# A skewness kernel on one core: fixed engine orders, 31 input transfers instead of 27, the last block's squares in PSUM, seven blocks closed together on GpSimd

## Chip, cores, metric

One Trainium2 chip (trn2), one core. The time is device microseconds (us) of one execution; the span is the time from the first to the last instruction in the trace. A program on one core has shown two kinds of run here: the runs of one kernel on one chip agree within 0.4%, except that one run of one experiment was 2% longer at a lower granted TensorE clock; it is left out of every comparison.

## The reference

```python
rows, cols = 1024, 8192                       # float32
mean = np.mean(x, axis=-1, keepdims=True)
std  = np.std(x, axis=-1, keepdims=True)
z    = (x - mean) / (std + 1e-8)
out  = np.mean(z ** 3, axis=-1)               # 1024 values
```

With the raw means m1, m2, m3 of x, x squared and x cubed, the result is (m3 - 3 m1 m2 + 2 m1^3) / (m2 - m1^2)^1.5, so one pass over x is enough. ("Moment" below is m2.)

## The kernel before

Eight blocks of 128 rows by 8192 columns stream in, each in several tiles, into SBUF, the core's large on-chip memory; PSUM is the smaller one, which also takes TensorE's results. ScalarE squares a tile and sums the squares (`accum_out`), VectorE multiplies the square by x and sums the cubes (such an instruction is called a cube below), TensorE transposes each 128x128 piece into one PSUM tile that adds them up, which gives the row sums.

```python
UNITS = [                       # widths of the transfers of each block: 27 in all
    [4096, 4096], [4096, 4096], [4096, 4096], [4096, 4096],
    [3584, 2304, 2304], [2304, 2304, 2048, 1536],
    [1664, 1792, 1920, 1664, 1152],
    [1024, 1024, 1152, 1280, 1408, 1152, 1152],
]
...
nc.sync.dma_start(out=xt, in_=xv[b, :, c0 : c0 + w])           # x tile, 8 buffers
nc.scalar.activation(out=sq, in_=xt[:, s:e], func=AF.Square, scale=s_scale,
                     accum_out=s2u[:, j : j + 1])
cube = sqpool.tile(...) if last_unit else sq                    # cube overwrites its square
nc.vector.scalar_tensor_tensor(out=cube, in0=sq, scalar=1.0, in1=xt[:, s:e],
                               op0=ALU.mult, op1=ALU.mult, accum_out=s3u[:, j : j + 1])
...
# blocks 0 to 5 are closed by six GpSimd steps while block 6 runs;
# blocks 6 and 7 by six small ScalarE steps each (close_on_act), then:
nc.gpsimd.tensor_tensor(out=rr, in0=var2, in1=expo[:, 0 : NB - F], op=ALU.pow)
nc.vector.tensor_reduce(out=num, in_=s3u[:, F * K :]..., axis=X_AXIS, op=ALU.add)
nc.vector.tensor_tensor(out=skew[:, F:NB], in0=num, in1=rr, op=ALU.mult)
nc.sync.dma_start(out=ov, in_=skew)
```

## Time and profile before

| | before |
|---|---|
| time, median of 3 runs | 91.64 us (91.53 to 91.65) |
| span of the profiled run | 89.73 us |
| last input tile landed | 83.56 us |
| result sent | 87.23 us |
| from there to the end of the span | 2.50 us |

I split the span at two places: until the last input tile has landed, from there until the result is sent (the tail), and the end. The first cut is read from the input transfers sent last: start, then time to landing. The second is the start of the output transfer in the timeline.

```profile
L140 SPq DMA_DIRECT2D x<-in_x_dram x1: 328/328/328, 76.1 to 76.1; - x1
...
DMA to landing us min/median/max: 7.5/7.5/7.5
...
87.23 0.35 SPq L193 DMA_DIRECT2D out_dram<-skew  x1
```

The first two lines say: sent at 76.1, landed 7.5 later, so 83.6. The prediction shows the other views (slices, chain, stretches, timeline) and how they are read.

### The profile page before, as it was taken

What the parts mean: (1) busy time and instruction counts of PE and PEld (TensorE: products, weight loads), DVE (VectorE), ACT (ScalarE), POOL (GpSimd) and SP (SyncE); (2) the same over time, 40 slices, a digit from 0 to 9 for tenths busy, and PEclk for the clock granted to TensorE, in tenths of its full rate; (3) what the DMA queues carried; (4) which work ended last, traced back from release to release, by engine and by line L of the source; (5) the groups of instructions that cost most, each with busy time, mean ns of one, the idle gap of its engine ahead of it and who ended that gap; (6) DMA issues with size and microseconds to landing.
All of it is one profiled execution on the core that took longest, in us unless ns stands there. A gap on an engine that the chain in (4) does not pass through costs nothing.

```text
span 89.7 us, 1368 instructions
## 1 busy us (share of the span) xinstructions
PE 64.9 (72%) x504; PEld 59.3 (66%) x504; DVE 72.7 (81%) x80; ACT 72.1 (80%) x106; POOL 11.3 (13%) x14
## 2 busy tenths in 40 slices
PE   0003999892882919989998988888987798969710
PEld 0003999791872909979897977877876787848500
DVE  1000498989999298995999999999999999999970
ACT  6003999699991999859898989978979898999950
POOL 3000000000000000000000000000005999900030
PEclk9999999999999997599999999999999999999998
DMA  3999999999999999999999999999999999994000
GB/s 117 351 424 438 424 431 431 431 431 424 446 416 431 424 438 424 424 438 427 415 409 418 419 427 419 421 415 419 409 414 417 404 413 411 421 412 161 0 0 2
DMA packets 4038, 33.64 MB, mean 375 GB/s; under 512 B 576, under 2 KB 576, under 8 KB 2240
## 3 DMA queue, kind: packets, MB, share of 16 engines
q1 hardware_dynamic: 4032, 33.56, 89.7%
q8 instruction: 4, 0.07, 0.3%
q14 instruction: 2, 0.02, 0.0%
HBM read 33.55 MB, written 0.00 MB: 374 GB/s over the span
## 4 chain that ended last, share of the span: by engine, by line
DMA 73%; ACT 13%; issue 5%; DVE 4%; SPq 1%; PE 1%; DVEq 0%; ACTq 0%
DMA x<-in_x_dram 73%; ACT sq L147 9%; DVE sq L152 3%; ACT sqps L147 1%; ACT same L159 1%; SPq L140 1%; PE s1ps L175 1%; ACT tsb L174 0%; ACT s3u L128 0%; ACT v L127 0%; ACT var L125 0%; DVE num L189 0%; ACT m1sq L124 0%; DVE skew L192 0%; ACT nm L126 0%
## 5 line engine op out<-in xcount | busy, mean ns | idle before, releaser
L152 DVE SCALAR_TENSOR_TENSOR sq<-sq,x 128x2048 f32<-128x2048 f32 (+9 forms) x35 | 70.7, 2071 | 13.4 <-ACT sq L147 13.3
L165 PE MATMUL tp<-ident,x 128*128 128x128 f32 x488 | 62.6, 288 | 17.3 <-DMA x<-in_x_dram 17.2
L165 PEld LDWEIGHTS tp<-ident,x 128*128 128x128 f32 x488 | 57.9, 150 | 20.9 <-DMA x<-in_x_dram 12.7
L147 ACT ACTIVATE sq<-x 128x2048 f32<-128x2048 f32 (+9 forms) x35 | 60.6, 1734 | 10.7 <-DMA x<-in_x_dram 9.9
L110 POOL TENSOR_TENSOR vara<-m2a,m1sqa 128x6 f32<-128x6 f32 x1 | 1.8, 1822 | 67.1 <-DVE m3a L99 67.1
L147 ACT ACTIVATION_READ_ACCUMULATOR sq<-x 128x1 f32 x35 | 6.5, 186 | 0.0
L175 PEld LDWEIGHTS s1ps<-onesn,tsb 128*128 128x128 f32 x16 | 2.4, 188 | 5.2 <-ACT tsb L174 5.2
L175 PE MATMUL s1ps<-onesn,tsb 128*128 128x1 f32 x16 | 3.1, 260 | 3.3 <-ACT tsb L174 3.3
L174 ACT COPY tsb<-tp 128x128 f32<-128x128 f32 x8 | 2.0, 256 | 2.0 <-PE tp L165 2.0
L114 POOL TENSOR_TENSOR rra<-vara,expo 128x6 f32<-128x6 f32 x1 | 3.3, 3267 | 0.0
L159 ACT ACTIVATE same<-x 128x1024 f32<-128x1024 f32 x3 | 3.1, 1041 | 0.0
L152 DVE DVE_READ_ACCUMULATOR sq<-sq,x 128x1 f32 x35 | 2.9, 83 | 0.0
L111 POOL TENSOR_TENSOR m1sq3a<-m1sq3a,vara 128x6 f32<-128x6 f32 x1 | 1.9, 1868 | 0.1
L77 ACT ACT_TABLE_LOAD x1 | 1.3, 1283 | 0.7 <-PEq L208 0.7
L187 POOL TENSOR_TENSOR rr<-var,expo 128x2 f32<-128x2 f32 x1 | 0.7, 702 | 7.7 <-ACT var L125 7.7
L152 DVE SCALAR_TENSOR_TENSOR cube<-sqps,x 128x1152 f32<-128x1152 f32 x1 | 1.4, 1350 | 0.0
L113 POOL TENSOR_TENSOR m3a<-m3a,m1sq3a 128x6 f32<-128x6 f32 x1 | 1.2, 1201 | 0.1
L147 ACT ACTIVATE sqps<-x 128x1152 f32<-128x1152 f32 x1 | 1.1, 1136 | 0.1
L115 POOL TENSOR_TENSOR skew<-m3a,rra 128x6 f32<-128x6 f32 x1 | 1.1, 1069 | 0.1
L124 ACT ACTIVATE m1sq<-s1ps 128x1 f32<-128x1 f32 x2 | 0.3, 171 | 0.5 <-PE s1ps L175 0.5
L75 DVE MEMSET onesn<- 128x1 f32 x1 | 0.1, 59 | 0.8 <-PEq L208 0.8
L112 POOL TENSOR_TENSOR m1sq3a<-m1sq3a,nm1a 128x6 f32<-128x6 f32 x1 | 0.7, 697 | 0.0
(28 smaller groups left out, 6.8 us busy)
## 6 DMA issues: line engine op xcount, KB each, us to landing
x<-in_x_dram SPq DMA_DIRECT2D x8, 2048.0 KB, 23.4
x<-in_x_dram SPq DMA_DIRECT2D x4, 1152.0 KB, 27.9
x<-in_x_dram SPq DMA_DIRECT2D x4, 576.0 KB, 8.6
x<-in_x_dram SPq DMA_DIRECT2D x1, 1792.0 KB, 33.0
x<-in_x_dram SPq DMA_DIRECT2D x2, 832.0 KB, 13.9
x<-in_x_dram SPq DMA_DIRECT2D x1, 1024.0 KB, 21.1
x<-in_x_dram SPq DMA_DIRECT2D x2, 512.0 KB, 10.0
x<-in_x_dram SPq DMA_DIRECT2D x1, 960.0 KB, 13.2
```

What stands on the lines that cost most here:

```text
L77: nc.scalar.activation(out=tiny, in_=onesn, func=AF.Square)
L110: g.tensor_tensor(out=var, in0=m2, in1=m1sq, op=ALU.subtract)
L111: g.tensor_tensor(out=m1sq3, in0=m1sq3, in1=var, op=ALU.add)
L113: g.tensor_tensor(out=m3, in0=m3, in1=m1sq3, op=ALU.add)
L114: g.tensor_tensor(out=rr, in0=var, in1=expo, op=ALU.pow)
L115: g.tensor_tensor(out=skew[:, 0:F], in0=m3, in1=rr, op=ALU.mult)
L147: nc.scalar.activation(out=sq, in_=xt[:, s:e], func=AF.Square, scale=s_scale, accum_out=s2u[:, j : j + 1],)
L152: nc.vector.scalar_tensor_tensor(out=cube, in0=sq, scalar=1.0, in1=xt[:, s:e], op0=ALU.mult, op1=ALU.mult, accum_out=s3u[:, j : j + 1],)
L159: nc.scalar.activation(out=same[:, 0:w_act], in_=xt[:, w - w_act : w], func=AF.Copy, scale=inv_n, accum_out=s1a[:, b : b + 1],)
L165: nc.tensor.matmul(out=tp, lhsT=xt[:, c * P : (c + 1) * P], rhs=ident, start=(k == 0 and c == 0), stop=(c0 == C and c == n - 1), is_transp ...
L174: nc.scalar.copy(out=tsb, in_=tp)
L175: nc.tensor.matmul(out=s1ps[:, b : b + 1], lhsT=tsb, rhs=onesn, start=True, stop=True)
```

## The change

Its intent: engine orders exactly as the program is written; smaller tiles earlier, so that VectorE is not late at the end; a last tile of 512 columns; no TensorE work given to ScalarE; squares of the last block and of the last tile before it in PSUM, where GpSimd can work beside VectorE; one closing for seven blocks. Cut to its core:

```diff
-    [4096, 4096],
-    [4096, 4096],
-    [3584, 2304, 2304],
-    [2304, 2304, 2048, 1536],
-    [1664, 1792, 1920, 1664, 1152],
-    [1024, 1024, 1152, 1280, 1408, 1152, 1152],
+    [3456, 1792, 2944],
+    [2944, 2304, 2944],
+    [2944, 2688, 2560],
+    [1920, 1920, 1792, 1536, 1024],
+    [1536, 1408, 1408, 1152, 1408, 1280],
+    [1152, 1280, 1408, 1280, 1280, 1280, 512],
-S1_ACT = {(0, 0): 1024, (1, 0): 1024, (2, 0): 1024}
+PSUM_FROM = (6, 5)
+PS_MAX, PS_BUFS = 1536, 2
-EARLY = 6
+EARLY = 7
+EARLY_AT = (7, 2)
...
+    ctx.enter_context(tc.manual_schedule(
+        engines={eng.PE, eng.Activation, eng.DVE, eng.Pool, eng.SP}))
...
+    cube = small("cube", PS_MAX)                       # one scratch tile for all PSUM cubes
...
+            if last_unit:
+                nc.scalar.copy(out=tsb, in_=tp)        # ahead of the last square
+                if (b, k) >= PSUM_FROM:
+                    sq = psq.tile([P, PS_MAX], FP, tag="psq", ...)[:, 0 : e - s]
                 nc.vector.scalar_tensor_tensor(
+                    out=cube[:, 0 : e - s] if (b, k) >= PSUM_FROM else sq,
                     in0=sq, scalar=1.0, in1=xt[:, s:e], ...
...
-    (closing of blocks 6 and 7 on ScalarE)
+    g.tensor_tensor(out=m2, in0=m2p, in1=s2u[:, j - 1 : j], op=ALU.add)
+    act(out=m1sq, in_=p1, func=AF.Square)
+    g.tensor_tensor(out=var, in0=m2, in1=m1sq, op=ALU.subtract)
+    g.tensor_tensor(out=rr, in0=var, in1=expo[:, 0:1], op=ALU.pow)
+    act(out=nm1, in_=p1, func=AF.Copy, scale=-3.0)
+    act(out=v3, in_=m1sq, func=AF.Identity, scale=1.0 / 3.0, bias=var)
+    nc.vector.tensor_reduce(out=num, in_=s3u[:, L * K : L * K + n_sl[L]], ...)
+    nc.vector.scalar_tensor_tensor(out=num, in0=v3, scalar=nm1, in1=num, op0=ALU.mult, op1=ALU.add)
+    nc.vector.tensor_tensor(out=skew[:, L:NB], in0=num, in1=rr, op=ALU.mult)
```

More of the change, by code (lines that the diff above doesn't have):

```diff
@@ L17, with _slices, _plan @@
     [4096, 4096],
-    [4096, 4096],
-    [4096, 4096],
-    [3584, 2304, 2304],
-    [2304, 2304, 2048, 1536],
-    [1664, 1792, 1920, 1664, 1152],
-    [1024, 1024, 1152, 1280, 1408, 1152, 1152],
+    [3456, 1792, 2944],
[4 more added lines that the diff above has]
+    [1152, 1280, 1408, 1280, 1280, 1280, 512],
 ]
-S1_ACT = {(0, 0): 1024, (1, 0): 1024, (2, 0): 1024}
+PSUM_FROM = (6, 5)
 SUB_MAX = 2304
+PS_MAX, PS_BUFS = 1536, 2
 X_BUFS = 8
 SQ_BUFS = 4
-EARLY = 6
-def _slices(w):
-    n = -(-w // SUB_MAX)
+EARLY = 7
+EARLY_AT = (7, 2)
+def _slices(w, most):
+    n = -(-w // most)
     step = -(-w // n // 128) * 128
     return [(s, min(s + step, w)) for s in range(0, w, step)]
+def _plan(b, k):
+    return _slices(UNITS[b][k], PS_MAX if (b, k) >= PSUM_FROM else SUB_MAX)
 @with_exitstack
@@ L45 @@
     nc = tc.nc
+    eng = mybir.EngineType
+    ctx.enter_context(tc.manual_schedule(
+        engines={eng.PE, eng.Activation, eng.DVE, eng.Pool, eng.SP}))
     P = nc.NUM_PARTITIONS
@@ L53 @@
     third = (1.0 / 3.0) ** 0.5
-    assert len(UNITS) == NB and all(sum(u) == C for u in UNITS)
-    nw = len(S1_ACT)
-    assert sorted(b for b, _ in S1_ACT) == list(range(nw)) and nw <= F
+    assert len(UNITS) == NB and all(sum(u) == C for u in UNITS) and F == L
     xv = x.rearrange("(p b) c -> b p c", b=NB)
     ov = out.rearrange("(p b) -> p b", b=NB)
-    K = max(sum(len(_slices(w)) for w in u) for u in UNITS) + 1
+    n_sl = [sum(len(_plan(b, k)) for k in range(len(u))) for b, u in enumerate(UNITS)]
+    K = max(n_sl)
     xpool = ctx.enter_context(tc.tile_pool(name="xp", bufs=X_BUFS))
@@ L67 @@
     onep = ctx.enter_context(tc.tile_pool(name="onep", bufs=1))
-    psum = ctx.enter_context(tc.tile_pool(name="ps", bufs=2, space=bass.MemoryType.PSUM))
+    psq = ctx.enter_context(tc.tile_pool(name="psq", bufs=PS_BUFS, space=bass.MemoryType.PSUM))
     psum1 = ctx.enter_context(tc.tile_pool(name="ps1", bufs=1, space=bass.MemoryType.PSUM))
@@ L83 @@
     nc.vector.memset(s3u, 0.0)
-    s1a = small("s1a", nw)
-    same = small("same", max(S1_ACT.values()))
+    cube = small("cube", PS_MAX)
     junk = small("junk", K)
@@ L89 @@
     skew = small("skew", NB)
-    s1ps = psum1.tile([P, NB], FP, tag="s1ps")
     m1a = small("m1a", F)
-    var2 = small("var2", NB - F)
-    Tsb = [small(f"tsb{i}", P) for i in range(2)]
+    tsb = small("tsb", P)
+    tp = psum1.tile([P, P], FP, tag="tp", name="tp")
+    s1ps = psum1.tile([P, NB], FP, tag="s1ps", name="s1ps")
+    act, g = nc.scalar.activation, nc.gpsimd
     def close_first_blocks():
@@ L103, in close_first_blocks @@
         m1sq, m1sq3, nm1 = small("m1sqa", F), small("m1sq3a", F), small("nm1a", F)
-        nc.scalar.copy(out=m1a[:, nw:F], in_=s1ps[:, nw:F])
-        nc.scalar.activation(out=m1sq, in_=m1a, func=AF.Square)
-        nc.scalar.activation(out=m1sq3, in_=m1a, func=AF.Square, scale=third)
-        nc.scalar.activation(out=nm1, in_=m1a, func=AF.Copy, scale=-3.0)
-        g = nc.gpsimd
+        act(out=m1sq, in_=m1a, func=AF.Square)
+        act(out=m1sq3, in_=m1a, func=AF.Square, scale=third)
+        act(out=nm1, in_=m1a, func=AF.Copy, scale=-3.0)
         var, rr = small("vara", F), small("rra", F)
@@ L115, in close_first_blocks @@
         g.tensor_tensor(out=skew[:, 0:F], in0=m3, in1=rr, op=ALU.mult)
-    def close_on_act(b):
-        m2, m1sq, nm1, v3 = (small(f"{t}_{b}", 1) for t in ("m2", "m1sq", "nm1", "v3"))
-        p1 = s1ps[:, b : b + 1]
-        var = var2[:, b - F : b - F + 1]
-        act = nc.scalar.activation
-        yield act(out=junk, in_=s2u[:, b * K : b * K + K], func=AF.Copy, accum_out=m2)
-        yield act(out=m1sq, in_=p1, func=AF.Square)
-        yield act(out=var, in_=m1sq, func=AF.Identity, scale=-1.0, bias=m2)
-        yield act(out=nm1, in_=p1, func=AF.Copy, scale=-3.0)
-        yield act(out=v3, in_=m1sq, func=AF.Identity, scale=1.0 / 3.0, bias=var)
-        yield act(
-            out=s3u[:, b * K + K - 1 : b * K + K], in_=v3, func=AF.Identity, scale=nm1
-        )
-    pending = iter(())
     for b, widths in enumerate(UNITS):
-        tp = psum.tile([P, P], FP, tag="tp", name=f"tp_{b}")
         c0 = 0
@@ L141 @@
             c0 += w
-            for s, e in _slices(w):
-                if last_unit:
-                    sq = psum1.tile([P, e - s], FP, tag="sqps", name=f"sqps_{s}")
-                else:
-                    sq = sqpool.tile([P, e - s], FP, tag="sq", name=f"sq_{b}_{k}_{s}")
-                nc.scalar.activation(
-                    out=sq, in_=xt[:, s:e], func=AF.Square, scale=s_scale,
-                    accum_out=s2u[:, j : j + 1],
-                )
-                cube = sqpool.tile([P, e - s], FP, tag="sq", name="cube") if last_unit else sq
-                nc.vector.scalar_tensor_tensor(
-                    out=cube, in0=sq, scalar=1.0, in1=xt[:, s:e],
-                    op0=ALU.mult, op1=ALU.mult, accum_out=s3u[:, j : j + 1],
-                )
-                j += 1
-            w_act = S1_ACT.get((b, k), 0)
-            if w_act:
-                nc.scalar.activation(
-                    out=same[:, 0:w_act], in_=xt[:, w - w_act : w], func=AF.Copy,
-                    scale=inv_n, accum_out=s1a[:, b : b + 1],
-                )
-            n = (w - w_act) // P
+            n = w // P
             for c in range(n):
@@ L169 @@
                 )
-            if k > 0:
-                next(pending, None)
-                next(pending, None)
-        tsb = Tsb[b % 2]
-        nc.scalar.copy(out=tsb, in_=tp)
-        nc.tensor.matmul(out=s1ps[:, b : b + 1], lhsT=tsb, rhs=onesn, start=True, stop=True)
-        if b == F - 2:
-            nc.vector.tensor_tensor(
-                out=m1a[:, 0:nw], in0=s1ps[:, 0:nw], in1=s1a, op=ALU.add
-            )
-        if b == F - 1:
-            close_first_blocks()
-        if b >= F:
-            pending = close_on_act(b)
@@ L184 @@
-    for _ in pending:
-        pass
-    rr = small("rr2", NB - F)
-    nc.gpsimd.tensor_tensor(out=rr, in0=var2, in1=expo[:, 0 : NB - F], op=ALU.pow)
-    num = small("num2", NB - F)
-    nc.vector.tensor_reduce(
-        out=num, in_=s3u[:, F * K :].rearrange("p (b c) -> p b c", c=K), axis=X_AXIS, op=ALU.add
-    )
-    nc.vector.tensor_tensor(out=skew[:, F:NB], in0=num, in1=rr, op=ALU.mult)
+            if last_unit:
+                nc.scalar.copy(out=tsb, in_=tp)
+            for s, e in _plan(b, k):
+                if (b, k) >= PSUM_FROM:
+                    sq = psq.tile([P, PS_MAX], FP, tag="psq", name=f"psq_{b}_{k}_{s}")[:, 0 : e - s]
+                else:
+                    sq = sqpool.tile([P, e - s], FP, tag="sq", name=f"sq_{b}_{k}_{s}")
+                act(
+                    out=sq, in_=xt[:, s:e], func=AF.Square, scale=s_scale,
+                    accum_out=s2u[:, j : j + 1],
+                )
+                nc.vector.scalar_tensor_tensor(
+                    out=cube[:, 0 : e - s] if (b, k) >= PSUM_FROM else sq,
+                    in0=sq, scalar=1.0, in1=xt[:, s:e],
+                    op0=ALU.mult, op1=ALU.mult, accum_out=s3u[:, j : j + 1],
+                )
+                j += 1
@@ new lines @@
+            if (b, k) == EARLY_AT:
+                nc.scalar.copy(out=m1a, in_=s1ps[:, 0:F])
+                close_first_blocks()
+            if b == L and k == len(widths) - 2:
+                m2p = small("m2p", 1)
+                act(out=junk[:, 0 : n_sl[L] - 1], in_=s2u[:, L * K : j], func=AF.Copy,
+                    accum_out=m2p)
+        if b < L:
+            nc.scalar.copy(out=tsb, in_=tp)
+        nc.tensor.matmul(out=s1ps[:, b : b + 1], lhsT=tsb, rhs=onesn, start=True, stop=True)
@@ new lines @@
+    p1 = s1ps[:, L : L + 1]
+    m1sq, nm1, v3, m2, var, rr, num = (
+        small(f"{t}_l", 1) for t in ("m1sq", "nm1", "v3", "m2", "var", "rr", "num")
+    )
+    g.tensor_tensor(out=m2, in0=m2p, in1=s2u[:, j - 1 : j], op=ALU.add)
[4 more added lines that the diff above has]
+    act(out=v3, in_=m1sq, func=AF.Identity, scale=1.0 / 3.0, bias=var)
@@ L193 @@
+    nc.vector.tensor_reduce(out=num, in_=s3u[:, L * K : L * K + n_sl[L]], axis=X_AXIS, op=ALU.add)
+    nc.vector.scalar_tensor_tensor(
+        out=num, in0=v3, scalar=nm1, in1=num, op0=ALU.mult, op1=ALU.add
+    )
+    nc.vector.tensor_tensor(out=skew[:, L:NB], in0=num, in1=rr, op=ALU.mult)
     nc.sync.dma_start(out=ov, in_=skew)
```

## The prediction

> **What bounds the kernel now.** I read the page first: the 40 slices, then the chain that ended last.
>
> ```profile
> DMA  3999999999999999999999999999999999994000
> GB/s 117 351 424 438 424 431 431 431 431 424 446 416 431 424 438 424 424 438 427 415 409 418 419 427 419 421 415 419 409 414 417 404 413 411 421 412 161 0 0 2
> DMA 73%; ACT 13%; issue 5%; DVE 4%; SPq 1%; PE 1%; DVEq 0%; ACTq 0%
> ```
>
> The 16 DMA engines are full from the second slice to the 36th: the 33.55 MB of x stream in without a gap, and no compute engine ever lets the queue run dry. So the span of 89.7 us is the stream plus what follows its last landing. The chain in order of time gives the cut between the two:
>
> ```profile
> 76.06 7.50 DMA x<-in_x_dram
> 83.56 0.02 issue
> 83.58 1.26 ACT sqps L147 x2
> 84.84 0.28 ACT tsb L174
> 85.12 0.04 issue
> 85.16 0.40 PE s1ps L175 x2
> ...
> 85.81 0.27 ACT var L125
> 86.09 0.02 issue
> 86.11 0.30 ACT v L127
> 86.42 0.02 issue
> 86.44 0.30 ACT s3u L128
> ...
> 87.04 0.16 DVE skew L192
> ```
>
> The last tile (1152 columns) lands at 83.56 us. From there it is 3.67 us until the result is sent (87.23 in the timeline), and 2.5 us more to the end of the span. In the tail, square, copy of the transposes, row sum and the five small ScalarE steps follow one another. Only those 3.67 us and the rate of the stream can change the time.
>
> Third, the rate against the width of the rows, from the stretches of ten microseconds (last column GB/s, the one before it the DMA share):
>
> ```profile
> 8.00:18.00 10.00, 9.42 (x58) 9.21 (x59) 7.47 (x7) 9.06 (x12) 0.00 (x0) 1.00 1.01 433
> 48.00:58.00 10.00, 9.00 (x80) 8.53 (x81) 10.00 (x11) 9.46 (x10) 0.00 (x0) 1.00 1.01 420
> 68.00:78.00 10.00, 8.65 (x74) 7.66 (x73) 10.00 (x15) 9.24 (x19) 9.38 (x6) 1.00 1.02 412
> ```
>
> The engines are equally full in all three, but with 4096-column tiles they move 433 GB/s, with 2304-column ones 420, and with those of 1024 to 1920 columns 412. A smaller transfer costs rate, though nothing waits.
>
> Fourth, the timeline of the end, for the pace of VectorE and for GpSimd:
>
> ```profile
> 68.26 1.88 DVE L152 SCALAR_TENSOR_TENSOR sq<-sq,x 128x1664 f32<-128x1664 f32 x1
> 68.38 1.82 POOL L110 TENSOR_TENSOR vara<-m2a,m1sqa 128x6 f32<-128x6 f32 x1 [67.07 <-DVE m3a L99]
> ...
> 79.72 1.36 DVE L152 SCALAR_TENSOR_TENSOR sq<-sq,x 128x1152 f32<-128x1152 f32 x1
> 81.00 1.49 DVE L152 SCALAR_TENSOR_TENSOR sq<-sq,x 128x1280 f32<-128x1280 f32 x1
> 82.42 1.62 DVE L152 SCALAR_TENSOR_TENSOR sq<-sq,x 128x1408 f32<-128x1408 f32 x1
> 85.24 1.35 DVE L152 SCALAR_TENSOR_TENSOR cube<-sqps,x 128x1152 f32<-128x1152 f32 x1
> 86.16 0.70 POOL L187 TENSOR_TENSOR rr<-var,expo 128x2 f32<-128x2 f32 x1 [7.68 <-ACT var L125]
> ```
>
> Starts of VectorE in a row give its pace: 1.28 us for 1152 columns, 1.42 for 1280, 1.54 for 1408, so about 1.04 ns a column and 0.08 us an instruction. ScalarE's squares, read the same way (starts at 78.45, 79.59, 80.86, 82.27), take 1.14, 1.27 and 1.41. A block of 8192 columns costs VectorE 9.0 us in six slices, and the stream 10.0: VectorE has 10% to spare, and at the end is as late as ScalarE's chain (its cube ends at 86.6, the chain at 86.7).
>
> **What the Trainium skill says.** "DMA: Bandwidth & Descriptors", section Bandwidth: a fixed cost per packet makes small rows slower, and 435 GB/s is the ceiling of the fabric; the trace agrees in kind, 433 falling to 412. The same page, "Queues, rings and completion order": each engine takes turns between queue rows packet by packet, so other traffic delays one engine of the 16; the page of before lists 4 packets of an instruction queue, 0.07 MB, and the stream fades out over two microseconds (161 GB/s in slice 37) instead of stopping at once, which fits, though no view here names the engine. "SBUF — State Buffer", "two separate sides": VectorE with two SBUF inputs and GpSimd exclude each other for whole instructions. The trace agrees: six-element subtractions took 1.8 us and ended 0.06 us after the VectorE instruction beside them (68.38+1.82=70.20 against 70.14). "ScalarE: Activation LUTs", "Step-by-step", holds PSUM the lower-latency destination; here 1136 ns against 1155 for 1152 columns, so 0.02 us, which I count as nothing.
>
> **The change part by part.**
> Stream. 27 input transfers become 31. A block of 4.194 MB takes 9.69 us at 433 GB/s in 2 transfers and 10.18 at 412 in about 5.9 (mean width 1390 in that stretch): 0.49 us for 3.9 transfers, 0.125 each. Four more: +0.5 us; the 420 of the middle stretch would make it a little different, so I take +0.45. Does the queue run dry? The eight transfers sent at once now hold 27,520 columns instead of 32,768. Tile k+8 leaves when tile k is cubed, some 6 us after landing at 4096 columns and 3 us at 1280; what is then still queued is never below about 7,000 columns, 8 us of stream. So no. The last landing moves from 83.56 to about 84.0.
>
> First blocks. Three partial sums on ScalarE go (1.04+0.19 us each); 24 transposes at about 0.12 us come to TensorE, 8 in each of three blocks: 64 x 0.12 = 7.8 us a block of ten. None is on the chain: worth 0. The single transpose buffer changes nothing either, since the row sum already stood between two blocks in TensorE's order and waited for ScalarE's copy.
>
> Tail, with the last landing as 0. Columns arrive every 1.24 ns, so tiles 2 to 5 of the last block land at -5.5, -3.9, -2.3 and -0.65. ScalarE: tile 2 until -4.1, four small steps of the early closing (0.5 us in the timeline before) until -3.6, tile 3 until -2.3, tile 4 until -0.95, tile 5 from -0.6 to 0.65, the partial second moment until 0.85. TensorE ends tile 5 at about 0.6 and the four transposes of the last tile at 1.15. The copy now goes ahead of the last square: 1.2 to 1.4. The square of 512 columns at 0.6 us: until 2.0. VectorE: tile 2 until -2.5, the two reductions 0.2, tile 3 until -0.85, tile 4 until 0.6, tile 5 (ready at 0.65) until 2.1, the last 512 columns 0.62: until 2.7; sum of the cubes until 2.9. Beside it TensorE's row sum is done at 1.85, ScalarE squares the mean at 2.05 to 2.2, GpSimd adds the moment (2.05 to 2.2) and subtracts (2.25 to 2.45), ScalarE's last step 2.5 to 2.8, GpSimd's power about 0.6 (0.70 for two columns): until 3.05. VectorE multiplies and adds 2.9 to 3.1 and once more until 3.3. The result leaves at 3.3 instead of 3.67: -0.35 us. Most of that is the last tile of 512 in place of 1152; GpSimd's hops and one more small VectorE step give part of it back.
>
> Sum: 91.64 + 0.45 - 0.35 = 91.7 us.
>
> **The rivals.**
> (a) GpSimd stays blocked. If a VectorE cube reading one input from PSUM shuts GpSimd out like one reading two from SBUF, each of the six closing steps ends only with a VectorE instruction, they run until about +3.5, and the last block's three GpSimd steps queue behind them; the result leaves at about 4.5, 92.9 us in all. For it: all six closing steps before were stretched (0.7 to 3.3 us). Against it: those stood beside cubes with two SBUF inputs; the only power beside a PSUM cube took 0.70, while the six-column one ran 1.2 us past the next VectorE boundary (74.18 to 75.38), which agrees with 0.45 us plus 0.12 a column and no blocking.
> (b) Which DMA engine is last. Landings stepped 4.87 us, then one of 6.1 (TensorE starts at 22.78 and 28.89) at an unchanged total rate, so single engines lose over a microsecond. If the changed program's instruction fetches fall otherwise, the last landing may be 0.6 us earlier or 1.2 later: 91.1 to 92.9.
> (c) The added rows cost nothing because the slowest engine sets the landing: 91.3. For it: 14.7 MB landed from 8.2 to 43.6 us and 16.8 MB from 43.6 to 83.6, 415 and 420 GB/s, no fall at all by landings.
> (d) The written order puts TensorE or ScalarE behind at a block's end. A copy waited 1.5 us for TensorE at 39 us before, at a reduced clock; such a wait is made up before the next blocks, so 0, unless it falls in the last block.
>
> **Range and chances.** (a) and (b) reach to 92.9 and (b) with (c) to 90.9. I take 90.9 to 92.5. Over 2% faster is under 89.8, which would take the whole fade of the stream away; over 2% slower is above 93.5, which needs (a) and (b) together or a queue run dry. Faster 0.04, within 0.91, slower 0.05.
>
> **What would show it.** Right: DMA slices at 9 throughout, the last landing near 84.0, rates about 425 in blocks 2 to 4, GpSimd's closing steps mostly under 0.5 us beside PSUM cubes, the result sent 3.1 to 3.6 us after the last landing, ScalarE's copy ahead of the last square. Wrong: a slice of DMA below 9 before the end (queue dry), GpSimd steps of over a microsecond after the seventh block (a), or a last landing outside 83.0 to 85.0 (b).

## The result, and the profile after

The changed kernel takes 92.34 us (92.27 to 92.40, 4 runs) against 91.63 (91.53 to 91.65, 4 runs): ratio 1.0079, 95% interval 1.0062 to 1.0097. A ratio is the mean time of one kernel's fast runs over that of the other's fast runs of the same rounds, so not quite the ratio of the medians quoted. The change is within 2%, and a small loss that is clear of noise.

The page's slices of the changed kernel, with its chain that ended last:

```profile
DMA  3999999999999999999999999999999999992000
GB/s 101 347 412 427 441 427 420 434 449 430 397 407 442 419 432 426 420 428 418 422 421 433 411 426 411 409 410 420 411 416 420 409 411 421 412 397 115 0 0 2
...
DVE 1%; issue 0%; DVEq 0%
```

The stream has no gap here either. The chain is the surprise: before it was 73% DMA, now it has only VectorE, 1% of the span, and in order of time it begins at 86.71 us. It is not that nothing came earlier: in the tail VectorE goes from cube to cube with no recorded wait for another engine, and a chain that is followed back by waits stops there. The last transfer and the timeline of the tail show what is going on:

```profile
L130 SPq DMA_DIRECT2D x<-in_x_dram x1: 328/328/328, 75.6 to 75.6; - x1
...
DMA to landing us min/median/max: 8.4/8.4/8.4
```

```profile
81.81 0.20 DVE L108 TENSOR_REDUCE m2a<-s2u 128x7 f32<-128x49 f32 x1
...
82.04 1.48 DVE L150 SCALAR_TENSOR_TENSOR cube<-psq,x 128x1280 f32<-128x1280 f32 x1
82.17 0.21 POOL L117 TENSOR_TENSOR vara<-m2a,m1sqa 128x7 f32<-128x7 f32 x1 [80.81 <-DVE m3a L108]
...
83.62 1.49 DVE L150 SCALAR_TENSOR_TENSOR cube<-psq,x 128x1280 f32<-128x1280 f32 x1
...
85.21 1.49 DVE L150 SCALAR_TENSOR_TENSOR cube<-psq,x 128x1280 f32<-128x1280 f32 x1
85.36 0.61 ACT L146 ACTIVATE psq<-x 128x512 f32<-128x512 f32 x1
...
86.80 0.69 DVE L150 SCALAR_TENSOR_TENSOR cube<-psq,x 128x512 f32<-128x512 f32 x1
...
87.54 0.16 DVE L178 TENSOR_REDUCE num_l<-s3u 128x1 f32<-128x7 f32 x1
87.82 0.22 DVE L179 SCALAR_TENSOR_TENSOR num_l<-v_l,nm_l,num_l 128x1 f32<-128x1 f32 x1
88.14 0.16 DVE L182 TENSOR_TENSOR skew<-num_l,rr_l 128x1 f32<-128x1 f32 x1
88.33 0.35 SPq L183 DMA_DIRECT2D out_dram<-skew  x1
```

Sent at 75.64, landed 8.4 later: 84.0, as predicted. The GpSimd subtraction took 0.21 us beside a cube from PSUM, where it took 1.82 before. The square of the last tile is done at about 86.1, yet its cube starts at 86.80: VectorE is the late one. Its 1280-column cubes last 1.48 to 1.49 us, as they did before, but start 1.58, 1.59 and 1.59 us apart, where before the next instruction started 1.42 us after a 1280-column one.

| us | before | after | difference |
|---|---|---|---|
| last landing | 83.56 | 84.0 | +0.44 |
| tail (landing to result sent) | 3.67 | 4.33 | +0.66 |
| result sent to end | 2.50 | 2.25 | -0.25 |
| span | 89.73 | 90.58 | +0.85 |

The times of the two profiled runs differ by as much (91.50 and 92.38).

### The profile page after: what moved, and what is told of

It is laid out like the page before. It is cut to its first block, busy times and chain, and to the rows that moved or that the text cites. A ratio compares the mean times of both kernels' runs of the same rounds, so it can differ in the third digit from the quotient of the medians.

```text
span 90.6 us, 1442 instructions
## 1 busy us (share of the span) xinstructions
PE 66.5 (73%) x528; PEld 60.2 (66%) x528; DVE 74.1 (82%) x92; ACT 69.1 (76%) x103; POOL 4.2 (5%) x16
## 5 line engine op out<-in xcount | busy, mean ns | idle before, releaser
L134 PE MATMUL tp<-ident,x 128*128 128x128 f32 x512 | 64.0, 282 | 16.0 <-DMA x<-in_x_dram 15.8
L150 DVE SCALAR_TENSOR_TENSOR sq<-sq,x 128x2048 f32<-128x2048 f32 (+9 forms) x34 | 62.0, 1872 | 12.4 <-ACT sq L146 12.3
L146 ACT ACTIVATE sq<-x 128x2048 f32<-128x2048 f32 (+9 forms) x34 | 53.5, 1575 | 14.4 <-DMA x<-in_x_dram 12.6
L150 DVE SCALAR_TENSOR_TENSOR cube<-psq,x 128x1280 f32<-128x1280 f32 (+3 forms) x8 | 11.1, 1390 | 0.7 <-ACT psq L146 0.2
L146 ACT ACTIVATE psq<-x 128x1280 f32<-128x1280 f32 (+3 forms) x8 | 9.3, 1161 | 0.9 <-DVE cube L150 0.5
L121 POOL TENSOR_TENSOR rra<-vara,expo 128x7 f32<-128x7 f32 x1 | 1.5, 1507 | 0.0
L146 ACT ACTIVATION_READ_ACCUMULATOR psq<-x 128x1 f32 x8 | 1.5, 188 | 0.0
L150 DVE DVE_READ_ACCUMULATOR cube<-psq,x 128x1 f32 x8 | 0.7, 84 | 0.0
L175 POOL TENSOR_TENSOR rr_l<-var_l,expo 128x1 f32<-128x1 f32 x1 | 0.6, 563 | 0.1
```

What stands on the lines that cost most here:

```text
L121: g.tensor_tensor(out=rr, in0=var, in1=expo, op=ALU.pow)
L134: nc.tensor.matmul(out=tp, lhsT=xt[:, c * P : (c + 1) * P], rhs=ident, start=(k == 0 and c == 0), stop=(c0 == C and c == n - 1), is_transp ...
L146: act(out=sq, in_=xt[:, s:e], func=AF.Square, scale=s_scale, accum_out=s2u[:, j : j + 1],)
L150: nc.vector.scalar_tensor_tensor(out=cube[:, 0 : e - s] if (b, k) >= PSUM_FROM else sq, in0=sq, scalar=1.0, in1=xt[:, s:e], op0=ALU.mult, ...
L175: g.tensor_tensor(out=rr, in0=var, in1=expo[:, 0:1], op=ALU.pow)
```

## Experiments

All gave correct results. "Before" beside a run is the kernel before on the same chip. The three pieces of every profiled run:

| run | time us | before us | ratio (95%) | last landing | tail | end |
|---|---|---|---|---|---|---|
| two scratch tiles | 91.88 | 91.59 | 1.0031 (1.0014-1.0048) | 83.8 | 3.9 | 2.25 |
| squares in SBUF | 94.01 | 91.59 | 1.0258 (1.0240-1.0277) | 83.8 | 6.1 | 2.24 |
| old transfers | 92.98 | 91.59 | 1.0147 (1.0125-1.0169) | 83.7 | 5.1 | 2.51 |
| new transfers in the kernel before | 91.98 | 91.59 | 1.0036 (1.0019-1.0052) | 84.1 | 4.0 | 2.24 |
| one cube tile in the kernel before | 92.43 | 91.61 | 1.0089 (1.0075-1.0103) | 83.9 | 4.5 | 2.49 |
| two scratch tiles, short end | 91.62 | 91.61 | 1.0003 (0.9990-1.0015) | 83.9 | 3.7 | 2.24 |
| 27 transfers, small end | 91.77 | 91.61 | 1.0012 (1.0000-1.0025) | 83.7 | 3.8 | 2.49 |
| six more transfers | 92.16 | 91.61 | 1.0061 (1.0047-1.0074) | 84.1 | 3.7 | 2.40 |
| best try | 91.38 | 91.54 | 0.9975 (0.9963-0.9988) | 83.5 | 3.5 | 2.49 |
| scheduler's order | 92.59 | 91.54 | 1.0108 (1.0093-1.0124) | 83.9 | 4.7 | 2.24 |

(Of the fourth row, five of six timed runs are fast, 91.87 to 92.08, and one, the first profile, is slow.)

**My theory before the first run.** All cubes from PSUM write one scratch tile, so each waits, on VectorE's own semaphore (a counter that finished instructions raise and others wait for), until the one before has finished; in place of overlapping with it, it starts 0.16 us later. The list of VectorE's instructions as built (names shortened) shows the wait: the first cube waits for its transfer and ScalarE, every later one for VectorE too.

```
cube <- psq_5_0, x_5   128x1280   waits DMA, Activation
cube <- psq_0_0, x_0   128x1152   waits DMA, DVE, Activation
```

The rivals: reading a square from PSUM is slower; ScalarE, held up by only two PSUM buffers, sets the pace; the transfers alone are the loss.

### Two scratch tiles in place of one

```diff
-    cube = small("cube", PS_MAX)
+    cubes = [small(f"cube{i}", PS_MAX) for i in range(2)]
...
-                    out=cube[:, 0 : e - s] if ...
+                    out=cubes[j % 2][:, 0 : e - s] if ...
```

> Edit: the eight cubes from PSUM go to two scratch tiles in turn instead of one; all else as in the changed kernel. Theory 1 (each cube waits for the one before it to be finished, because all write one scratch): the starts of neighbouring 1280-column cubes go from 1.58 us apart back to 1.42, the last cube starts 0.4 to 0.5 us earlier against the last landing, and the time falls from 92.34 to 91.8-91.9. Rival (reading the square from PSUM is what slows a cube): starts stay 1.58 us apart, 92.3. Rival (ScalarE waiting for one of two PSUM buffers sets the pace): the starts stay apart, with idle time put down to ScalarE, 92.2-92.4.

91.88 us, as theory 1 had it. The ratio falls from 1.0079 to 1.0031, some 0.44 us. VectorE in the timeline:

```profile
81.87 1.48 DVE L150 SCALAR_TENSOR_TENSOR cube<-psq,x 128x1280 f32<-128x1280 f32 x1
...
83.28 1.49 DVE L150 SCALAR_TENSOR_TENSOR cube<-psq,x 128x1280 f32<-128x1280 f32 x1
...
84.79 1.49 DVE L150 SCALAR_TENSOR_TENSOR cube<-psq,x 128x1280 f32<-128x1280 f32 x1
```

Squares still lie in PSUM, and the starts are 1.41 and 1.51 us apart, and the last cube follows at 86.21 after 1.42: reading PSUM was not the cause. The first two cubes from PSUM in this trace still share a tile (their j is 47 and 49, both odd), and they start 1.58 us apart (75.33 and 76.91), although the second's square was done at 76.64. The 1.51, 0.09 too long, is what the second rival has of the truth: the square of that tile waited 0.27 us for a cube to free one of the two buffers.

### Squares in SBUF again

```diff
-PSUM_FROM = (6, 5)
+PSUM_FROM = (9, 0)
```

> Edit: no square in PSUM, so the last block's cubes overwrite their squares in SBUF, as in all other blocks; closing on GpSimd as in the changed kernel. Shared port (a GpSimd instruction waits for a cube with two SBUF inputs): the early closing's GpSimd steps take about 1.4 us each instead of 0.2, they run past the last cube, the last block's GpSimd steps queue behind them, the result is sent about 1.5 us later than in the changed kernel: 93.5-94.5. If GpSimd were not shut out: starts of the cubes 1.42 us apart and the time as with two scratch tiles, 91.8.

94.01 us, within the range given for a shared port. The GpSimd steps in the timeline:

```profile
81.98 1.42 POOL L117 TENSOR_TENSOR vara<-m2a,m1sqa 128x7 f32<-128x7 f32 x1 [80.63 <-DVE m3a L108]
...
83.48 1.33 POOL L118 TENSOR_TENSOR m1sq3a<-m1sq3a,vara 128x7 f32<-128x7 f32 x1
...
88.54 0.19 POOL L172 TENSOR_TENSOR m_l<-m2p,s2u 128x1 f32<-128x1 f32 x1
```

The same instructions that take 0.20 us beside cubes from PSUM last until the cube beside them ends. The early closing is over at 88.58 instead of 84.96, and the last block's first GpSimd step starts at 88.54 instead of 86.16. Against the run with two scratch tiles, which has none of the waits either, squares in PSUM are worth 2.1 us to this closing. VectorE's starts here are 1.40 to 1.42 apart, which again speaks for the wait and not for any cost of the cube itself.

### The old transfers in the changed kernel

```diff
-    (31 widths of the change)
+    (27 widths of before)
-PSUM_FROM = (6, 5)
+PSUM_FROM = (6, 4)
```

> Edit: the changed kernel with the 27 transfers of before (PSUM from the last tile of the seventh block on, as now). Cost per transfer: the last landing comes back from 84.0 to 83.5-83.7 us. Against it the last tile is 1152 columns instead of 512, some 0.4 us more after the landing. Expected 92.2-92.4; if the widths alone were the loss, 91.6; if transfers cost nothing, 92.7.

A miss: 92.98 us. The landing came back to 83.7 as expected, but the tail grew from 4.3 to 5.1 us, not by 0.4. VectorE's last cubes started at 83.36, 85.08 and 86.54 and ended at 87.90: after the last landing it still had nearly three wide tiles of 1152 to 1408 columns to do, each with its wait. I had added up a longer last tile and overlooked the three ahead of it. So in the changed kernel the new widths are worth 0.6 us (1.0147 against 1.0079).

### The new transfers in the kernel before

```diff
-    (27 widths)
+    (31 widths of the change)
```

> Edit: the kernel before with the 31 transfers of the change, nothing else. Cost per transfer: last landing 83.9-84.1 us instead of 83.56; the last tile of 512 columns shortens what follows by about 0.4 us: 91.5-91.8. If the transfers alone were the loss of the change: 92.3.

91.98 us, a little above the range given: 0.36% slower than before.

> A second look at the kernel before with the 31 transfers, whose profile fell in the slow state; only for a trace in the fast state. Last landing 83.9-84.1 us; from there to the sending of the result 3.4 to 3.7 us, set by VectorE's cubes of 1280 columns and not by ScalarE's chain; 91.9-92.0 in all.

92.18 us in one run, result sent 4.0 us after a landing at 84.1. The landing is as expected; the tail is not. VectorE in that trace:

```profile
77.53 1.36 DVE L152 SCALAR_TENSOR_TENSOR sq<-sq,x 128x1152 f32<-128x1152 f32 x1 [0.40 <-ACT sq L147]
...
79.62 1.49 DVE L152 SCALAR_TENSOR_TENSOR sq<-sq,x 128x1280 f32<-128x1280 f32 x1 [0.72 <-ACT sq L147]
```

It stood idle 0.4 and 0.7 us at the start of the last block, because the closing of the block before lies between ScalarE's squares (two small steps at 76.12 and 76.19, and three from 77.38 to 78.24); then its cubes run without a pause to 87.5, where it ended at 86.6 before. The idle time is shown; that it is the whole of the missing gain is my reading of it.

### One cube tile in the kernel before

```diff
+    one_cube = small("one_cube", 1408)
...
-                cube = sqpool.tile(...) if last_unit else sq
+                cube = one_cube[:, 0 : e - s] if b == L else sq
```

> Edit: the kernel before, where the seven cubes of the last block go to one scratch tile instead of back into their squares (the last one had a tile of its own); squares stay where they were. Theory (a cube waits for the one before it when both write one tile): starts of the last block's cubes move apart by 0.15 us each, VectorE ends 0.8 to 1.0 us later than 86.6 and sends the result with it, 92.3-92.6. Rival (only PSUM as a source slows a cube): 91.6, as before.

92.43 us, 0.82 more than the kernel before. Squares are in SBUF here (but for the last one), the order is the old one, and only the output tile of seven cubes changed:

```profile
80.16 1.36 DVE L153 SCALAR_TENSOR_TENSOR one_cube<-sq,x 128x1152 f32<-128x1152 f32 x1
...
81.62 1.49 DVE L153 SCALAR_TENSOR_TENSOR one_cube<-sq,x 128x1280 f32<-128x1280 f32 x1
...
83.21 1.63 DVE L153 SCALAR_TENSOR_TENSOR one_cube<-sq,x 128x1408 f32<-128x1408 f32 x1
```

The next start follows 1152 and 1280 columns after 1.46 and 1.59 us; before it was 1.28 and 1.42. That is 0.17 to 0.18 us for each wait. Removing the wait in one kernel and adding it in the other agree, so the cause of this part is shown.

### Two scratch tiles and a shorter end

```diff
+    act(out=t3, in_=v3, func=AF.Identity, scale=nm1)
     nc.vector.tensor_reduce(out=num, ...)
-    nc.vector.scalar_tensor_tensor(out=num, in0=v3, scalar=nm1, in1=num, op0=ALU.mult, op1=ALU.add)
-    nc.vector.tensor_tensor(out=skew[:, L:NB], in0=num, in1=rr, op=ALU.mult)
+    nc.vector.scalar_tensor_tensor(out=skew[:, L:NB], in0=num, scalar=t3, in1=rr,
+                                   op0=ALU.add, op1=ALU.mult)
```

> Edit: two scratch tiles as in the first run, and the last block's end in two VectorE steps instead of three (ScalarE multiplies the two small factors, VectorE adds and multiplies in one instruction). VectorE's dependent small steps stand 0.3 us apart, each ends the path: 0.3 us less than with two scratch tiles alone, 91.5-91.6. If they are hidden behind GpSimd's power or ScalarE: 91.8-91.9.

91.62 us: the ratio falls from 1.0031 to 1.0003. One VectorE step that waits for the step ahead of it is worth about 0.26 us at the very end, though it works for 0.16 to 0.22.

### 27 transfers with a small end

```diff
-    (31 widths)
+    [4096, 4096], [4096, 4096], [4096, 4096], [3456, 2432, 2304], [2944, 2688, 2560],
+    [2944, 2688, 2560], [1920, 1920, 1792, 1536, 1024],
+    [1408, 1408, 1408, 1280, 1152, 1024, 512]
-PSUM_FROM = (6, 5)
+PSUM_FROM = (7, 3)
```

> Edit: as the run with two scratch tiles and the short end, with 27 transfers: six of 4096 columns, then 3456 down to 1024, a last one of 512; PSUM squares only from the fourth tile of the last block on. Cost per transfer of 0.1 us: last landing about 83.5 us instead of 84.0, so 91.1-91.3, faster than the kernel before by 0.3 to 0.5 us. If the number of transfers does not matter: 91.5-91.6.

A miss: 91.77 us, no better than with 31. Against the run before this one the landing came earlier by 0.3 us (83.95 to 83.67) and not by 0.5, and the end after the result was sent grew from 2.24 to 2.49 us, which takes nearly all of it back. The tail grew by 0.15 us although the last cube started 0.3 us earlier (86.01): the last VectorE step now waited for ScalarE's product of the two small factors, which follows GpSimd's steps.

```profile
87.23 0.22 DVE L181 SCALAR_TENSOR_TENSOR skew<-num_l,t_l,rr_l 128x1 f32<-128x1 f32 x1 [0.33 <-ACT t_l L179]
```

So here the hops between engines end the tail, and not VectorE's cubes. Across all runs this end goes with the number of transfers and not with the kernel: 2.24 to 2.25 us in every kernel with 31 inputs and one output, 2.48 to 2.51 in every one with 27 and one, 2.40 with 33 and one (so it does not fall steadily with the number); the output itself lands 1.4 us after sending before and after. What makes the difference stays open.

### Six more transfers in the kernel before

```diff
-    [4096, 4096], [4096, 4096], [4096, 4096],      # blocks 1 to 3
+    [2048, 2048, 2048, 2048], [2048, 2048, 2048, 2048], [2048, 2048, 2048, 2048],
```

> Edit: the kernel before with the second to fourth blocks in four transfers of 2048 columns each, 33 in all instead of 27; the last four blocks unchanged. Cost of 0.10 to 0.125 us per transfer: last landing 84.2-84.3 us instead of 83.56, same tail, 92.2-92.4. If the number of transfers does not set the landing: 91.6.

92.16 us, just under the range of the first theory. The last four blocks, and so the tail, are those of before:

```profile
L140 SPq DMA_DIRECT2D x<-in_x_dram x1: 328/328/328, 76.8 to 76.8; - x1
...
DMA to landing us min/median/max: 7.3/7.3/7.3
```

Landed at 76.84 + 7.3 = 84.1, 0.57 us later than before: in this one pair of traces 0.1 us of landing for each transfer of 128 rows, where traces with the same transfers differ by up to 0.3 us. The tail is 3.7 as before, and the end 0.1 shorter. That the time fits is in part luck: only about 0.3 us of its 0.56 lie in the span (90.16 us in the mean of the timed runs, 89.86 before). The rest lies outside it, 2.05 us instead of 1.77; no other run shows that, and its cause stays open.

### The scheduler's order in the changed kernel

```diff
-    ctx.enter_context(tc.manual_schedule(
-        engines={eng.PE, eng.Activation, eng.DVE, eng.Pool, eng.SP}))
```

> Edit: the changed kernel without the fixed engine orders, all else the same. The scheduler puts the early closing ahead of the last block's squares and cubes, and the copy of the transposes behind the last square. The two reductions (0.23 us of VectorE) and four ScalarE steps (0.5 us) leave the tail, the row sum comes 0.5 us later but ends before VectorE does: 92.0-92.3. If the order as written was a gain: over 92.5. If it was nothing: 92.34.

A miss of the main expectation: 92.59 us, 0.3% slower than the order as written, as named for the case that this order was a gain. The early closing moved ahead of the last block, as I had read from the orders as built, but it delayed the block's start, because its first step on ScalarE waits for the row sum of the block before and stands ahead of the first square:

```profile
76.11 0.17 ACT L155 COPY m1a<-s1ps 128x7 f32<-128x7 f32 x1 [0.47 <-PE s1ps L163]
```

That square started at 76.17 instead of 75.56, the second-tile cube at 79.00 instead of 78.53, and from there the cubes ran at the pace of the one scratch tile (79.00, 80.59, 82.31, 83.91, 85.49). A reduction taken out of the tail gains nothing when the same chain of cubes starts later by more (0.47 us against 0.2). The order as written is a small gain of the change.

### A version from what was learned

```diff
-PSUM_FROM = (6, 5)
+IN_PSUM = {(7, 1), (7, 2), (7, 3), (7, 6)}
-EARLY_AT = (7, 2)
+EARLY_AT = (7, 0)
     last block: [1536, 1408, 1280, 1152, 1152, 1024, 640], 27 transfers, two scratch tiles, short end
-    act(out=v3, in_=m1sq, func=AF.Identity, scale=1.0 / 3.0, bias=var)
+    act(out=v3, in_=m1sq, func=AF.Identity, scale=-2.0 / 3.0, bias=m2)
```

> Edit, on the run with 27 transfers and a small end: the early closing after the first tile of the last block instead of the fourth step, so that its two VectorE reductions and four ScalarE steps leave the tail; squares in PSUM only for tiles 1, 2, 3 and 6 of the last block, so that no square waits for one of the two PSUM buffers in the tail; last block 1536 down to 640; the last multiplier taken from the second moment and not from the variance, one GpSimd step less ahead of ScalarE. Last landing as there, 83.7; VectorE's last cube ends 0.3 to 0.5 us earlier: 91.3-91.5, below both kernels. If the tail is set by ScalarE's and GpSimd's hops instead: 91.6-91.8.

91.38 us against 91.54, ratio 0.9975 (0.9963 to 0.9988): faster than both kernels, by a quarter of a per cent over the one before.

```profile
87.05 0.35 SPq L184 DMA_DIRECT2D out_dram<-skew  x1
```

The output transfer in the timeline: the result leaves at 87.05, 0.18 earlier than before, after a landing at 83.5 like that of before. Which of the edits gave how much of it was not taken apart.

## Why the prediction was right, and where it was not

92.34 lies inside the range of 90.9 to 92.5 and inside 2%, but towards its upper edge, 0.6 us above the point. By its steps:

1. *The stream bounds the kernel and never runs dry.* Right; the slices show it, before and after, and from 22 to 52 us the changed kernel moved 423 GB/s, near the 425 named for blocks 2 to 4.
2. *The last landing moves from 83.56 to about 84.0, 0.45 us for four transfers.* Right for this pair of traces, 84.0; over all, too large. With 27 transfers the last landing lies at 83.50 to 83.86 us (five traces, mean 83.65), with 31 at 83.78 to 84.07 (six traces, the slow one left out, mean 83.93): 0.28 us for four, 0.07 each, where 0.125 had been assumed from the rates. The means speak against rival (c), that rows cost nothing by landings. But the end is shorter with 31 by about as much (step 5): landing and end together are 86.15 us on average with 27 and 86.17 with 31. By these averages the four transfers cost the time next to nothing, and the loss is that of the tail.
3. *GpSimd works freely beside a cube from PSUM.* Right; rival (a) is refuted (0.20 us a step), and the run with squares in SBUF shows the 2 us that it would have cost. One step of over a microsecond, which the prediction had named as a sign of (a), did occur: the power of seven columns took 1.51 us. But in the run with squares in SBUF it took 1.50, there after the last cube (86.80 to 88.30), so this is its own length; the prediction's 0.45 us plus 0.12 a column would have made it 1.29.
4. *"The result leaves at 3.3 instead of 3.67: -0.35 us."* This is the term that failed: it left 4.33 us after the landing, outside the 3.1 to 3.6 that it had named as a sign of being right, so the tail changed by +0.66. Three parts of that step were mis-sized. "VectorE's pace" was read from cubes that overwrite their own squares, and taken for cubes that all write one scratch: each start came 0.16 us later than the step had it, and two scratch tiles gave 0.43 us of tail back. The three dependent VectorE steps of the end were put at 0.2 us each, and took 0.83 together, from the end of the last cube and its accumulator read at 87.50 to 88.33; one fewer gave 0.26 back. And "tile 2 until -2.5" was -2.2 (81.81 against 84.0): the tile was taken up 0.2 us later against the last landing than reckoned, its square took 0.1 more, and every cube after it inherited both. These add to the 1.0 us by which the step missed.
5. *The end after sending stays 2.5 us.* Not said, but assumed in the sum; it became 2.25, which took back 0.25 of the 1.10 us that landing and tail had lost. This was luck: without it the time would have been about 92.6 us, outside the range. And the range was as wide as it was for rivals (a) to (c); no rival named VectorE's pace.
6. *Rival (d), the order as written puts an engine behind, and rival (b), which DMA engine is last.* (d): the order is a gain of about 0.27 us, not a loss. (b): the last landing varies by 0.3 us among the six traces with the 31 transfers of the change, and no run tells single DMA engines apart, so this stays open.

By the ratios, which come from different rounds, the transfers alone, in the old kernel, cost 0.36% of the 0.79%, and the single scratch tile, taken out of the changed kernel, gives 0.48% back. These parts can't simply be added: in the changed kernel the new widths are a gain of 0.68% (1.0147 to 1.0079), in the old one a loss. What orders, PSUM and closing together are worth by themselves was not isolated.

## What to carry to other kernels

A scratch output that nobody reads is still a dependence: where one engine writes it again and again, give it two tiles, or each instruction pays for its predecessor's end (0.16 to 0.18 us here), and no view shows it as a wait for another engine; compare distances between starts, not durations. In a kernel bound by a stream, the tail is set by the slower engine's whole backlog at the last landing, so reckon it from several tiles back and not from the last tile. Before cutting transfers smaller for a shorter tail, compare whole times and not landings: here each cost 0.07 to 0.1 us of landing, but with 31 transfers the end of the program was shorter by about the same.

## What the Trainium skill lacked or had wrong

- "VectorE: DVE Perf Modes", "Rules for kernel authors", says of chained operations not to fuse for speed and to minimize the number of operations, not of semaphores. Here the number of operations stayed the same and one semaphore wait of VectorE on itself cost 0.16 to 0.18 us each time it stood between two cubes: 0.82 us in all in the kernel before, 0.43 us of tail in the changed one. The page gives no time for how far two instructions without such a wait overlap: here the next cube started 0.07 us before the end of the one ahead of it.
- "GPSIMD Engine Reference", section 3.1, has figures of `tensor_tensor` for 2048 columns only, and the page has none for a power. A `tensor_tensor` of 1 to 7 columns took 0.19 to 0.21 us here when not shut out, a power 0.56 us for one column and 1.51 for seven.
- No page that I read has it: the time from sending the result to the end of the program was 2.24 to 2.25 us with 32 transfers in all, 2.48 to 2.51 with 28 and 2.40 with 34.
